# An instruction order put together stretch by stretch from twelve turns of a scheduler, in place of the best of eight turns

## The chip, the cores and the metric

The kernel runs on one core of a Trainium2 chip. The metric is the device time of one execution in microseconds (us). Three runs of the kernel before took 1519.48, 1521.61 and 1521.72 us; their median, 1521.61 us, is the time before.

## The reference

A two-layer encoder on 512 tokens of width 1024, all in float32. Each layer adds a normed token mixer and a normed SwiGLU to the stream:

```python
def reference(x, ...):
    for layer in range(DEPTH):                      # DEPTH = 2
        h = rms_norm(x, norm_mix_pre[layer])
        if layer % N_MIXERS == 0:
            h = neighbourhood_attention(h, ...)     # 8 x 64 token grid, window 8 x 16
        else:
            h = dilated_attention(h, ...)           # three (window, dilation) groups, merged
        x = x + rms_norm(h, norm_mix_post[layer])
        h = rms_norm(x, norm_ffn_pre[layer])
        x = x + rms_norm(swiglu(h, ...), norm_ffn_post[layer])
```

Layer 0 uses neighbourhood attention, layer 1 dilated attention; both have 16 heads of 64.

## The kernel before, in words

All large products are split into a high and a low part of float32r: `mm3` (L374 to L376) issues three matrix products for each wanted one. The projections of queries, keys, values and of the gate and up matrices go through a scheme with seven block products in place of eight (`Seven`, `Values`), whose sums are made by POOL and DVE and whose splits into high and low are made by ACT (L362) and DVE (L363).

The stages follow each other as: norm and transposes of the input; mixer 0 (eight pairs of heads; 0 to about 230 us); its output product `yo`; gate and up of layer 0 (`gu`, 22 units); the product down (`yd`); norm and transposes; the values of mixer 1 (`vd`), then eight pairs of heads of mixer 1 with three query/key units each (`pp_d`; about 730 to 1137 us); its output product; gate, up and down of layer 1.

Beside the float32r products, TensorE (PE) has 128x128 transposes (L748 to L755 in mixer 0, L1322 in mixer 1, L596 for operands) and a third kind: plain float32 products on half of the array. These are the products of probabilities and values (L766 in mixer 0; L1331 and L1337 in mixer 1) and the scores of two of the three dilated groups (L1264). Each of them shows in the profile as two records. An unbroken run of such half-array products on PE is called a **visit** below.

The order of the work is not the order of the Python code. After the whole program has been recorded, the class `Order` takes all instructions, gives each a cost in ns on its engine (`_cost`), links them by what they read and write and by the buffers they share (`link`), and computes an order for each of the five queues (PE, ACT, DVE, POOL, SP) by list scheduling (`run`). `run` knows three kinds of PE work and a cost `SWITCH` for a change of kind, and for 1000 ns of rank it stays with the kind it has (`stay`). `pin` makes a number of turns: a pass forward by rank gives start times, a pass backward from these gives new ranks, and so on. It keeps the order whose computed end is the earliest and pins it: each queue's instructions are chained one after the other (`add_manual_dep`). What runs on the chip is this fixed order on each queue. An engine whose next instruction is not ready waits, whatever else stands behind it.

SP issues the loads. In mixer 1 it also carries the merge weights of each pair of heads: a small array is written to `sw` in device memory (L1194) and read back into another layout by four small reads (L1196) each time. Between these stand the loads of later weights (L358), which wait until their buffer is free.

The lines that the steps below speak of, in short (L766 in `window_pv`, L1331 and L1337 in `values`, L1264 in `scores_b`, the others in `swapped` and in `Order.run`):

```python
pe.matmul(o[64 * hd:64 * hd + 64, q0:q0 + nq], v[:, kt, c:c + 64], pts[hd][:, p0:p0 + nq], ...)        # L766
rw = slice(64 * hd, 64 * hd + 64)
pe.matmul(ss[hd][:, f0:f0 + P], qf[rw, block(c)], kf[rw, block(c)], start=True, stop=True)             # L1264
pe.matmul(o[64 * hd:64 * hd + 64, q0:q0 + nq], vg[0][:, kt, c0:c0 + 64], pts[j, 0, hd][:, p0:p0 + nq], ...)  # L1331
nc.sync.dma_start(d[:, :4 * n], in_)                                                                   # L1194
for k in range(4):
    nc.sync.dma_start(out_[32 * k:32 * k + 32].rearrange(...), d[:, n * k:n * k + n].rearrange(...))   # L1196
...
heap = min((q for q in heaps[e] if q), key=lambda q: q[0])          # run: the lowest rank that is ready
for q in heaps[e][3:] if kind == 3 else heaps[e][kind:kind + 1]:
    if e == 0 and q and q[0][0] < heap[0][0] + self.stay:           # PE: the kind that it has, if near enough
        heap = q
```

Of the kernel before, what the change touches and what calls it, by code (L numbers as in the profile page):

```python
# [129 lines left out]
class Order:  # L130
# [145 lines left out]
                now = min(q[0] if q is wake else q[0][0] for q in (wake, pending) if q)  # L276
        return starts, order, max(s + max(c[1], c[4] and LANDING + c[4] / RATE) for s, c in zip(starts, self.costs))

    def pin(self, tc, times):
        rank, best = list(range(len(self.all))), None  # L280
        for _ in range(times):
            starts, order, end = self.run(rank, False)
            if best is None or end < best[0]:
                best = end, order
            starts, _, end = self.run([-s - c[1] for s, c in zip(starts, self.costs)], True)
            rank = [end - s - c[0] for s, c in zip(starts, self.costs)]
        for q in best[1]:
            for m, n in zip(q, q[1:]):
                tc.add_manual_dep(self.all[n], self.all[m].name,
                                  mybir.DependencyInfo(mybir.DependencyClass.NoSync, mybir.DependencyReason.DATA),  # L290
                                  reason="order")
        return best[0]


@with_exitstack
def encoder_kernel(ctx: ExitStack, tc: tile.TileContext, a: dict, out: bass.AP):
# [817 lines left out]
    for j in range(PAIRS):  # L1114
# [3 lines left out]
        q = next(q_).rearrange("p (h t) -> p h t", h=2)  # L1118
# [226 lines left out]
    order = [3 * j + g for j in range(PAIRS) for g in orders[j]]  # L1345
# [36 lines left out]
    for n, i in enumerate(order):  # L1382
# [7 lines left out]
        if g == 0:  # L1390
            q = q_.rearrange("p (h t) -> p h t", h=2)
# [34 lines left out]
              for n, lo, hi, o, c, side in arenas]  # L1426
    order = Order(tc.nc.cur_bb.bb.instructions)
    order.link(tags, places, extra)
    order.pin(tc, 8)


def _blocks(w, cols):
# [79 lines left out]
```

## Time and profile before

| | |
|---|---|
| median of three runs | 1521.61 us |
| profiled execution, its own time | 1517.54 us |
| span in that profile | 1515.8 us |
| PE busy | 1462.6 us, 96% of the span |
| DVE, ACT, POOL busy | 79%, 59%, 39% |
| share of the chain that ended last: PE, ACT, DVE, DMA | 70%, 4%, 4%, 2% |

The span is what the instructions cover; the execution's own time is 1.74 us more, and that execution was 4.07 us under the median of the runs. PE counts as busy while a matrix product is in its pipeline, so the busy share hides small losses between the starts of products; the timeline, which gives each start, shows them.

### The profile page before, as it was taken

What the parts mean: (1) busy time and instruction counts of PE and PEld (TensorE: products, weight loads), DVE (VectorE), ACT (ScalarE), POOL (GpSimd) and SP (SyncE); (2) the same over time, 40 slices, a digit from 0 to 9 for tenths busy, and PEclk for the clock granted to TensorE, in tenths of its full rate; (3) what the DMA queues carried; (4) which work ended last, traced back from release to release, by engine and by line L of the source; (5) the groups of instructions that cost most, each with busy time, mean ns of one, the idle gap of its engine ahead of it and who ended that gap; (6) DMA issues with size and microseconds to landing.
All of it is one profiled execution on the core that took longest, in us unless ns stands there. A gap on an engine that the chain in (4) does not pass through costs nothing.

```text
span 1515.8 us, 27980 instructions
## 1 busy us (share of the span) xinstructions
PE 1462.6 (96%) x10788; PEld 1355.0 (89%) x10788; DVE 1190.3 (79%) x1884; ACT 895.4 (59%) x1787; POOL 597.4 (39%) x484
## 2 busy tenths in 40 slices
PE   7999998999999999999999999999998999999997
PEld 7988876999999788999999988989986999999786
DVE  5389976898888789797578667877747988887876
ACT  4467764555555557544468667877764654555564
POOL 4356754543330001676464455454306433330001
PEclk9999999999999999999999999999998999999999
DMA  5356575756462774545334776672647232322762
GB/s 180 115 206 161 173 245 202 193 173 201 153 157 77 238 227 148 204 154 160 132 126 169 175 200 186 186 189 72 211 153 223 84 112 84 112 84 91 259 220 91
DMA packets 82118, 247.26 MB, mean 163 GB/s; under 512 B 18816, under 2 KB 29056, under 8 KB 79936
## 3 DMA queue, kind: packets, MB, share of 16 engines
q1 hardware_dynamic: 70064, 180.32, 35.7%
q0 software_dynamic: 11776, 64.88, 16.1%
q8 instruction: 85, 1.39, 0.4%
q14 instruction: 49, 0.40, 0.1%
q10 hardware_dynamic: 144, 0.26, 0.0%
HBM read 223.31 MB, written 68.26 MB: 192 GB/s over the span
## 4 chain that ended last, share of the span: by engine, by line
PE 70%; ACT 4%; DVE 4%; DMA 2%; issue 2%; POOL 1%; SPq 0%; POOLq 0%; DVEq 0%; ACTq 0%
PE gu L375 10%; PE gu L374 10%; PE gu L376 10%; PE pp_d L374 4%; PE pp_d L376 4%; PE pp_d L375 4%; PE yd_s L376 3%; PE yd_s L374 3%; PE yd_s L375 3%; PE yd_pp L375 2%; PE yd_pp L376 2%; PE yd_pp L374 2%; PE vd L374 2%; PE vd L376 2%; PE vd L375 2%
## 5 line engine op out<-in xcount | busy, mean ns | idle before, releaser
L375 PE MATMUL gu<-rxc,h_a 128*128 128x256 f32 x352 | 101.4, 288 | 2.9 <-DVE rxc L599 2.8
L376 PE MATMUL gu<-rxc,l_a 128*128 128x256 f32 x352 | 101.0, 287 | 0.2 <-DVE l_a L363 0.2
L374 PE MATMUL gu<-rxc,h_a 128*128 128x256 f32 x352 | 101.2, 290 | 0.0
L375 PE MATMUL gu<-rxa,h_b 128*128 128x256 f32 x352 | 99.8, 284 | 0.8 <-DVE rxa L599 0.8
L374 PE MATMUL gu<-rxa,h_c 128*128 128x256 f32 x352 | 100.3, 285 | 0.0
L374 PE MATMUL gu<-rxa,h_b 128*128 128x256 f32 x352 | 99.9, 284 | 0.0
L376 PE MATMUL gu<-rxa,l_b 128*128 128x256 f32 x352 | 99.7, 283 | 0.0
L375 PE MATMUL gu<-rxa,h_c 128*128 128x256 f32 x352 | 99.5, 283 | 0.0
L376 PE MATMUL gu<-rxa,l_c 128*128 128x256 f32 x352 | 99.4, 283 | 0.0
L442 POOL TENSOR_TENSOR fg<-fg 128x512 f32<-128x512 f32 x24 | 38.1, 1586 | 121.1 <-DVE l_a L363 105.6
L362 ACT ACTIVATE rxc<-hid 128x512 fp32r<-128x512 f32 (+1 forms) x84 | 49.3, 592 | 60.9 <-PE yd_pp L375 37.9
L442 POOL TENSOR_TENSOR r_gu<-r_gu 128x512 f32<-128x512 f32 x20 | 30.8, 1540 | 108.9 <-DVE l_a L363 94.4
L442 POOL TENSOR_TENSOR r_d<-r_d 128x512 f32<-128x512 f32 x24 | 36.8, 1533 | 92.3 <-DVE l_ad L363 38.6
L363 DVE TENSOR_TENSOR rxc<-hid,rxc 128x512 fp32r<-128x512 f32 (+1 forms) x84 | 53.7, 647 | 23.8 <-ACT rxc L362 22.0
L375 PEld LDWEIGHTS gu<-rxc,h_a 128*128 128x128 f32 x352 | 68.8, 196 | 3.5 <-DVE rxc L599 3.5
L1232 ACT ACTIVATE ap<-ap 128x256 f32<-128x256 f32 x128 | 63.8, 504 | 11.2 <-DVE ap L1231 11.0
L374 PEld LDWEIGHTS gu<-rxc,h_a 128*128 128x128 f32 x352 | 69.0, 197 | 0.5 <-ACT rxc L598 0.5
L376 PEld LDWEIGHTS gu<-rxc,l_a 128*128 128x128 f32 x352 | 68.8, 196 | 0.5 <-DVE l_a L363 0.5
L375 PEld LDWEIGHTS gu<-rxa,h_b 128*128 128x128 f32 x352 | 67.5, 192 | 1.0 <-DVE rxa L599 1.0
L572 POOL DMA_DIRECT2D hid<-g_ffn_post x2 | 1.2, 617 | 170.0 <-DVE rxc L363 170.0
L374 PEld LDWEIGHTS gu<-rxa,h_c 128*128 128x128 f32 x352 | 67.5, 192 | 0.8 <-DVE fg L838 0.4
L374 PEld LDWEIGHTS gu<-rxa,h_b 128*128 128x128 f32 x352 | 67.5, 192 | 0.2
(602 smaller groups left out, 6254.5 us busy)
## 6 DMA issues: line engine op xcount, KB each, us to landing
wsum<-wd POOLq DMA_DIRECT2D x24, 1408.0 KB, 11.5
r_d<-dil_qk SPq DMA_DIRECT2D x48, 512.0 KB, 4.5
fg<-wg SPq DMA_DIRECT2D x24, 512.0 KB, 3.8
fg<-wu SPq DMA_DIRECT2D x24, 512.0 KB, 5.1
wsum<-wsum POOLq DMA_DIRECT2D x8, 1408.0 KB, 7.7
raw<-wsum SPq DMA_DIRECT2D x22, 512.0 KB, 4.7
r_gu<-wg SPq DMA_DIRECT2D x20, 512.0 KB, 3.7
r_gu<-wu SPq DMA_DIRECT2D x20, 512.0 KB, 4.5
```

What stands on the lines that cost most here:

```text
L362: act.activation(h, src, AF.Copy)
L363: dve.tensor_sub(l, src, h.bitcast(F32))
L374: i = pe.matmul(o, s[0], m[0], start=start, stop=False, skip_group_check=True)
L375: pe.matmul(o, s[0], m[1], start=False, stop=False, skip_group_check=True)
L376: pe.matmul(o, s[1], m[0], start=False, stop=stop, skip_group_check=True)
L442: self.added = e[0].tensor_add(q[0], q[0], q[2])
L572: queue.dma_start(g, bass.AP(tensor=row.tensor, offset=row.offset, ap=[[0, P], [1, D]]))
L1232: act.activation(pr[:, f], pr[:, f], AF.Exp, bias=st[:, c:c + 1], scale=-1.0, accum_out=st[:, c + 2:c + 3])
```

## The change

`pin` makes twelve turns in place of eight and keeps, of each but the first, the computed end, the ranks, the start times and the order. It takes the turn with the earliest end as the base. Then it goes through the program in stretches of 50000 ns of the base's computed time. For each stretch and each other turn it replaces the ranks of the instructions that start in the stretch by that turn's ranks (moved by the median difference, so that they fit to the rest), runs the scheduler forward once more, and keeps the new order where its computed end is earlier. Instructions, tiles, costs and links stay as they are.

```diff
-    def pin(self, tc, times):
-        rank, best = list(range(len(self.all))), None
-        for _ in range(times):
+    def pin(self, tc, times, span):
+        rank, found = list(range(len(self.all))), []
+        for n in range(times):
             starts, order, end = self.run(rank, False)
-            if best is None or end < best[0]:
-                best = end, order
+            if n:
+                found.append((end, rank, starts, order))
             starts, _, end = self.run([-s - c[1] for s, c in zip(starts, self.costs)], True)
             rank = [end - s - c[0] for s, c in zip(starts, self.costs)]
-        for q in best[1]:
+        found.sort(key=lambda f: f[0])
+
+        best, rank, base, order = found[0]
+        for lo in np.arange(0.0, max(base), span):
+            part = [k for k, s in enumerate(base) if lo <= s < lo + span]
+            for _, other, _, _ in found[1:]:
+                mixed, shift = list(rank), float(np.median([rank[k] - other[k] for k in part]))
+                for k in part:
+                    mixed[k] = other[k] + shift
+                _, new, end = self.run(mixed, False)
+                if end < best:
+                    best, rank, order = end, mixed, new
+        for q in order:
...
-    order.pin(tc, 8)
+    order.pin(tc, 12, 5e4)
```

What it comes to: the order before is that of the eighth turn, and the base of the new one is the twelfth, with pieces of other turns in twelve of its thirty stretches. Of PE's 10388 products 8019 keep their place in the row, and no other moves by more than 100 places; of ACT's 1544 instructions 992 keep theirs, of DVE's 1676 it is 1112, of POOL's 480 it is 415, of SP's 467 it is 398. On PE the rows differ, with equal pieces between, at what was 76 to 220 us, 265 to 297, 604 to 626, 776 to 1138, 1176 to 1198 and 1327 to 1400 us of the profile; elsewhere they are the same. PE makes 82 visits in the order before (20 in mixer 0, 62 in mixer 1) and 67 in the new one (16 and 51). By the lines in a visit: L766 alone 20 and now 16, L1331 alone 13 and 9, L1337 alone 13 and 7, L1264 alone 23 and 21, mixed 13 and 14.

In the rows below, the line numbers of the changed kernel are greater by 12.

**PE, end of mixer 0.** `o_6` is the value product of the seventh pair, `ta`/`tb` are its neighbour's transposes, `s_15` the last head's scores. Before:

```order
L766 MATMUL o_6_2278<-ap_255,apv 64x192
L766 MATMUL o_6_2278<-ap_255,apv 64x256
L753 MATMUL tb_13_2267<-ident,ap_255 128x128
L754 MATMUL tb_13_2267<-ident,ap_255 128x128
L755 MATMUL tb_13_2267<-ident,ap_255 128x64
L766 MATMUL o_6_2278<-ap_255,apv 64x256 x2
L715 MATMUL s_15_1_2404<-rxc 128x256
L716 MATMUL s_15_1_2404<-rxc 128x256
L715 MATMUL s_15_1_2404<-rxc 128x256
L716 MATMUL s_15_1_2404<-rxc 128x256
L766 MATMUL o_6_2278<-ap_255,apv 64x256
L766 MATMUL o_6_2278<-ap_255,apv 64x192 x2
```

Now:

```order
L765 MATMUL tb_13_2267<-ident,ap_255 128x128
L766 MATMUL tb_13_2267<-ident,ap_255 128x128
L767 MATMUL tb_13_2267<-ident,ap_255 128x64
L727 MATMUL s_15_1_2404<-rxc 128x256
L728 MATMUL s_15_1_2404<-rxc 128x256
L727 MATMUL s_15_1_2404<-rxc 128x256
L728 MATMUL s_15_1_2404<-rxc 128x256
L778 MATMUL o_6_2278<-ap_255,apv 64x192 x2
L778 MATMUL o_6_2278<-ap_255,apv 64x256 x4
L778 MATMUL o_6_2278<-ap_255,apv 64x192 x2
```

The eight products of `o_6` stood in four visits (the first, of one product, is ten rows ahead of what is shown), and stand in one now, behind the scores.

**PE, mixer 1.** `pp_d` are the query/key products, `o_0` the values of the first pair, `sb` the scores of dilated groups. Before:

```order
L374 MATMUL pp_d_8940<-rxb_6344,h_bd_9073 128x256
L1337 MATMUL o_0_8478<-ap_6475 64x4x32
L1264 MATMUL sb_1_1_8832<-ap_6475 128x128
L1337 MATMUL o_0_8478<-ap_6475 64x4x32
L1264 MATMUL sb_0_0_9139<-ap_6475 128x128
L375 MATMUL pp_d_8940<-rxb_6344,h_bd_9073 128x256
```

Now, some 30 rows earlier:

```order
L388 MATMUL pp_d_8940<-rxa,l_ad_8955 128x256
L1276 MATMUL sb_0_1_8831<-ap_6475 128x128
L1276 MATMUL sb_1_1_8832<-ap_6475 128x128
L1349 MATMUL o_0_8478<-ap_6475 64x4x32 x8
L386 MATMUL pp_d_8781<-rxb_6344,h_bd_8901 128x256
```

Left-over products that stood by themselves have moved into the visit ahead.

**SP, mixer 1, fourth pair of heads.** `r_d` are weight buffers, `sw` the small array of the merge weights. Before:

```order
L358 DMA r_d_10213<-dil_qk 128x1024
L1194 DMA sw_6478<-ap_6475 128x16
L358 DMA r_d_10213<-dil_qk 128x1024
L1196 DMA ap_6475<-sw_6478 32x4x4 x4
L358 DMA r_d_10443<-dil_qk 128x1024 x2
L1194 DMA sw_6480<-ap_6475 128x8
```

Now:

```order
L370 DMA r_d_10213<-dil_qk 128x1024 x2
L1206 DMA sw_6478<-ap_6475 128x16
L370 DMA r_d_10443<-dil_qk 128x1024
L1208 DMA ap_6475<-sw_6478 32x4x4 x4
L370 DMA r_d_10443<-dil_qk 128x1024
L1206 DMA sw_6480<-ap_6475 128x8
```

One load of the next weights has moved from behind the group of four small reads to ahead of it. At six of the groups of mixer 1 at least one load has moved ahead in this way.

## Rows read from the trace of the kernel before

**Rows 1.** The page of the profile: the span, each engine's busy time, and the TensorE clock that was granted, in 40 slices (9 is 90% of full speed or more).
```profile
span 1515.8 us, 27980 instructions
PE 1462.6 (96%) x10788; PEld 1355.0 (89%) x10788; DVE 1190.3 (79%) x1884; ACT 895.4 (59%) x1787; POOL 597.4 (39%) x484
PEclk9999999999999999999999999999998999999999
```

**Rows 2.** Busy time of each engine in stretches of the span: the stretch, then us busy (and instructions) of PE, weight loads, DVE, ACT and POOL, the granted clock as a share of full speed, the share of the DMA engines, GB/s.
```profile
85.00:220.00 135.00, 131.14 (x950) 113.38 (x951) 122.72 (x298) 99.40 (x237) 90.77 (x108) 1.00 0.63 195
300.00:500.00 200.00, 199.85 (x1632) 198.07 (x1632) 175.51 (x226) 103.26 (x180) 61.49 (x41) 1.00 0.51 152
604.00:626.00 22.00, 21.35 (x180) 21.01 (x181) 19.03 (x24) 12.14 (x20) 15.16 (x11) 1.00 0.49 168
777.00:1000.00 223.00, 221.16 (x1834) 203.96 (x1834) 167.27 (x368) 156.12 (x400) 116.63 (x97) 1.00 0.65 183
1000.00:1137.00 137.00, 136.01 (x1071) 120.52 (x1069) 94.55 (x217) 103.18 (x263) 44.74 (x41) 1.00 0.52 157
1156.00:1172.40 16.40, 8.99 (x43) 7.89 (x42) 15.33 (x14) 6.80 (x12) 16.40 (x13) 0.69 0.59 225
1327.00:1400.00 73.00, 73.00 (x595) 72.11 (x594) 62.03 (x88) 38.91 (x67) 13.54 (x8) 1.00 0.26 85
```

**Rows 3.** What PE waited for: engine, tile and line that waited <- what it waited for: us in total, times, the longest.
```profile
PE tr_o L596 <- DVE rxc L599: 9.7, 2, 5.1
PE tr_a L596 <- DVE ea L589: 8.0, 1, 8.0
...
PE o L766 <- ACT ap L756: 0.8, 2, 0.4
...
PE t L1322 <- DVE ap L1323: 0.3, 1, 0.3
```

**Rows 4.** The timeline of PE around three visits of mixer 1: one product of L1331, two of L1337, twelve of L1337 (2, 4 and 24 records): start in us, us until the last end, what. The start-to-start times matter, since ends overlap.
```profile
828.76 0.28 PE L374 MATMUL pp_d<-rxa,h_cd 128*128 128x256 f32 x1
828.97 0.65 PE L1331 MATMUL o<-ap 128*64 128x256 f32 x2
...
829.77 0.28 PE L376 MATMUL pp_d<-rxa,l_cd 128*128 128x256 f32 x1
...
892.36 0.28 PE L376 MATMUL pp_d<-rxb,l_bd 128*128 128x256 f32 x1
892.48 0.28 PE L374 MATMUL pp_d<-rxb,h_bd 128*128 128x256 f32 x1
892.69 0.44 PE L1337 MATMUL o<-ap 128*64 128x128 f32 x4
...
893.28 0.28 PE L376 MATMUL pp_d<-rxb,l_bd 128*128 128x256 f32 x1
...
1033.97 0.28 PE L376 MATMUL pp_d<-rxa,l_cd 128*128 128x256 f32 x1
1034.18 1.53 PE L1337 MATMUL o<-ap 128*64 128x128 f32 x24
...
1035.86 0.28 PE L375 MATMUL pp_d<-rxa,h_cd 128*128 128x256 f32 x1
```

**Rows 5.** The same for two visits of mixer 0, one of seven products (14 records) and one of a single product (2 records).
```profile
201.15 0.39 PE L375 MATMUL yo<-l_wo,rxa 128*128 128x512 f32 x1
201.38 0.39 PE L376 MATMUL yo<-h_wo,rxa 128*128 128x512 f32 x1
201.70 1.73 PE L766 MATMUL o<-ap,apv 128*64 128x192 f32 x14
203.36 0.27 PE L748 MATMUL ta<-ident,ap 64*128 64x64 f32 x1
203.56 0.33 PE L749 MATMUL ta<-ident,ap 128*128 128x128 f32 x1
...
211.61 0.39 PE L376 MATMUL yo<-rxa 128*128 128x512 f32 x1
211.93 0.54 PE L766 MATMUL o<-ap,apv 128*64 128x192 f32 x2
212.40 0.27 PE L748 MATMUL ta<-ident,ap 64*128 64x64 f32 x1
212.60 0.33 PE L749 MATMUL ta<-ident,ap 128*128 128x128 f32 x1
```

**Rows 6.** The timeline of SP's queue in mixer 1: a load with a group of small reads issued right behind it, and the group of the fourth pair with the loads behind it.
```profile
835.57 0.33 SPq L358 DMA_DIRECT2D r_d<-dil_qk  x1
835.99 2.31 SPq L1196 DMA_DIRECT2D ap<-sw  x4
...
941.16 1.92 SPq L1196 DMA_DIRECT2D ap<-sw  x4
943.19 0.84 SPq L358 DMA_DIRECT2D r_d<-dil_qk  x2
```

**Rows 7.** DMA issues, KB each and median us from issue to landing: from the page, the loads of `r_d` over the whole span; from the stretch 805 to 840 us, the small reads that were issued at 835.99 us.
```profile
r_d<-dil_qk SPq DMA_DIRECT2D x48, 512.0 KB, 4.5
...
ap<-sw SPq DMA_DIRECT2D x4, 1.0 KB, 1.6
```

More of the change, by code (lines that the diff above doesn't have):

```diff
@@ L291, in pin @@
                                   reason="order")
-        return best[0]
+        return best
 @with_exitstack
```

## The prediction, as recorded before the changed kernel ran

> **What bounds the kernel now.** I read the page first. PE is busy for 1462.6 of 1515.8 us and the granted clock is near full in all slices [rows 1]; no other engine is above 79%. So the time is PE's row of products plus the places where PE waits. The stretches show where those places are: in gate and up (300 to 500 us, 1327 to 1400 us) PE idles for 0.15 us and not at all, while it idles for 3.86 us of 135 in mixer 0, 0.65 of 22 between the layers, 1.84 of 223 and 0.99 of 137 in mixer 1 [rows 2]. The largest single losses are transposes of operands that wait for DVE, 9.7 us in two waits and 8.0 us in one [rows 3]. The second of the two long ones lies in the stretch 1156 to 1172.4 us, where PE is busy for 8.99 of 16.4 us and the mean clock is 0.69, a mix of the two levels 2.4 and 1.2 GHz after PE had idled [rows 2]. The reader is to see that the new order leaves these transposes and the products around them in the same sequence, so that I count nothing there. What is left for a new order is small: 7.34 us of idle in the four stretches it changes (3.86 + 0.65 + 1.84 + 0.99), and what PE loses without showing idle, by changing its kind of work. For that I went to the timeline of PE and read start-to-start times.
>
> **The term that is certain: 15 visits fewer.** A product of 128x256 follows the one before it after 0.12 us (892.36 to 892.48) [rows 4]. Around a visit it is more. From the last full product ahead of a visit to the second one behind it I subtract the two full products themselves, 0.24 us.
> Two products of L1337: 892.48 to 893.28 is 0.80, less 0.24 is 0.56 us. Twelve of them: 1033.97 to 1035.86 is 1.89, less 0.24 is 1.65 us [rows 4]. The ten more cost 1.09, so 0.109 each, and 0.56 - 2 x 0.109 = 0.34 us belong to the visit and not to its products.
> In mixer 0, seven products of L766: 201.38 to 203.56 is 2.18 us; a single one: 211.61 to 212.60 is 0.99 us [rows 5]. The six more cost 0.198 each. The single one's 0.99 holds a `yo` product of 0.23 (as 201.15 to 201.38), a small transpose of 0.20 (212.40 to 212.60, as 203.36 to 203.56) and its own 0.198, which leaves 0.36 us for the visit.
> A single product of L1331: 828.76 to 829.77 is 1.01, less 0.24 is 0.77 us [rows 4]; it has 256 columns as most of L766's have, so by 0.198 for the product 0.57 us are the visit's.
> L1264 alone I did not price by a pair of its own; I take L1337's 0.34, the low end.
> By the lines of the visits that go: 4 x 0.36 (L766) + 4 x 0.57 (L1331) + 6 x 0.34 (L1337) + 2 x 0.34 (L1264), less 0.34 for the one mixed visit more, is 1.44 + 2.28 + 2.04 + 0.68 - 0.34 = **6.1 us**. The bounds are 15 x 0.34 = 5.1 and 15 x 0.57 = 8.6 us. The same products are still done; only the entering and leaving goes.
>
> **The term that is open: waits.** The new order does not make ACT, DVE or POOL faster, and their rows have moved too (552 of ACT's 1544 instructions, 564 of DVE's 1676). Where PE reaches a product sooner than its operand is there, the gain turns into a wait. In mixer 1 PE idles for 0.8% and 0.7% of the two stretches, and its transposes of probabilities waited for 0.3 us in all [rows 2, 3], so most of the gain there should stay. In mixer 0 PE idles for 2.9%, and a value product waited for ACT's copy [rows 2, 3]; this is the stretch in which DVE is busy for 122.72 of 135 us. There I take the gain of the four visits, 1.4 us, as given back. From both sides: if the idle of the four changed stretches went too, 7.3 us more would be gained; if each of the gains met a wait, all 6.1 would be lost.
>
> **Edits at nothing.** In 1327 to 1400 us only products of one kind change places and PE is busy for 73.00 of 73 us; the cover is that the operands lie ready, and if it goes the loss is a wait like those above. At 604 to 626 us some transposes change places with value products; PE idles there for 0.65 us, which bounds a gain, and a loss of that size is my bound on the other side. At 265 to 297 and 1176 to 1198 us transposes of the third and fourth token blocks move by a few products among `gu` products; by the same argument nothing.
> On SP, one load or more has moved ahead of the small reads of the merge weights at six places. Behind them wait DVE's weights and ACT's scaling, and behind these PE's transposes. The row shows that a group of small reads issued 0.42 us behind a 512 KB load had landed 1.6 us after its issue [rows 6, 7], so the load does not hold the reads back much once it is issued. What can hold them is the load's own wait for its buffer: at the fourth pair it was issued at 943.19, right behind reads issued at 941.16 [rows 6], so in the new row the reads could go out up to 2.0 us later. PE's wait of 0.3 us in all at these transposes [rows 3] is why I count nothing for it.
> The Trainium skill ("DMA: Bandwidth & Descriptors", "Queues, rings and completion order") says that on each DMA engine the descriptors of one queue are consumed in ring order, which speaks against this move: by it the reads would start behind the whole load. With the median of 4.5 us of such a load [rows 7] six places would be late by 27 us together before any cover; the 1.6 us above do not bear that out, and I go by the row.
>
> **The sum.** 6.1 - 1.4 = 4.7 us less. Against the profiled execution, 1517.54 us, that gives 1512.8. That execution lies 4.07 us under the median of the runs, and the forecast is for the median of runs: 1521.6 - 4.7 = **1516.9 us**.
>
> **Rivals.** A change of under 0.2%, 3.0 us, can hardly be told from none by measurements of this kernel.
> (a) *The gain turns into waits.* The twelve turns and their pieces are compared by computed costs, which may not be those of the chip; for it speaks that every third row of ACT and DVE has moved, against it that PE idles so little in mixer 1. If at least 1.7 us more of the 4.7 are given back, the result is within 0.2%; if all, 1521.6 us. Chance 0.28.
> (b) *The idle goes too.* In mixer 0 the order gathers the value products behind the scores, and a wait of 0.4 us for ACT ahead of a value product [rows 3] may go with it. Keeping all 6.1 and winning the larger part of 7.3 us, say 4, gives 1511.5 us. Chance 0.12.
> (c) *Merge weights late: slower.* At the six groups the reads go out 2.0 us later each [rows 6], 12 us in all, and PE's transposes of these pairs then wait for the scaled probabilities. With the 6.1 us won this is 5.9 us more, 1527.5 us. It decides from 9.1 us of such waits on (6.1 + 3.0). For it speaks that the load of the fourth pair went out right behind the reads [rows 6], which leaves open since when its buffer had been free; against it, the 0.3 us of waits before [rows 3]. Were the queue's ring order to hold the reads for the whole load, as the skill's page would have it, the loss would be larger still. Chance 0.12.
>
> **How the numbers follow.** My forecast, 1514 to 1518.6 us, has 0.48, (a) 0.28, (b) 0.12, (c) 0.12. The range runs from 1510 to 1524 us: it takes in (b) at 1511.5, the forecast with the visits at either bound (5.1 and 8.6), and (a) with a small loss; most of (c) stays out, which with the tails is no more than 2 in 10. Faster by over 0.2% are the forecast and (b): 0.60. Within 0.2% is (a): 0.28. Slower is (c): 0.12.
>
> **What would show it.** In the new profile, visits of one product should be rarer in the timeline between 85 and 1137 us, and the starts around a single one as far apart as before. PE's last product of the output of mixer 1 should start some 4 to 6 us earlier, with most of it won after 777 us; from there on both profiles should run alike, the waits for operands of 5 us and the low clock after them included. In the list of waits, `t` at L1322 should stay under 1 us; if it shows several us, with DVE's weights waiting longer for `sw`, (c) is at work. If visits have gone and PE's idle in the changed stretches has grown by as much, it is (a). If PE's stretch from 1198 us on starts later than before, the forecast is wrong.

## The result and the profile after

The changed kernel takes 1522.59 us (median of 20 runs; 1518.88 to 1525.75) against 1518.51 us for the kernel before on the same chip (20 runs; 1515.15 to 1521.76). The ratio is 1.0025 with a 95% interval of 1.0016 to 1.0035: about 4 us slower, where 4.7 us faster was forecast. The profiled execution of the changed kernel took 1523.31 us, its span is 1521.5 us. Line numbers of the changed kernel are 12 higher than those before, below `pin`.

The page of the changed kernel, span and PE's busy time [rows 1 before], with DVE, ACT and POOL:
```profile
span 1521.5 us, 27984 instructions
PE 1458.8 (96%) x10788; PEld 1353.5 (89%) x10788; DVE 1190.7 (78%) x1884; ACT 895.0 (59%) x1787; POOL 590.3 (39%) x484
```
With the same products PE is busy for 3.8 us less than before (1462.6), and the span is 5.7 us longer, so its waits have grown by more. Three of the stretches that [rows 2] showed, now:
```profile
85.00:220.00 135.00, 129.51 (x943) 112.31 (x944) 125.03 (x296) 96.29 (x227) 85.11 (x108) 1.00 0.63 187
...
777.00:1000.00 223.00, 215.28 (x1802) 200.80 (x1801) 166.52 (x354) 156.31 (x398) 114.04 (x95) 0.98 0.63 179
1000.00:1137.00 137.00, 135.10 (x1061) 121.58 (x1060) 94.50 (x229) 103.52 (x266) 46.82 (x44) 1.00 0.55 165
```
PE's idle has grown from 3.86 to 5.49 us in mixer 0, and from 1.84 to 7.72 us in 777 to 1000 us, where the mean clock has also fallen to 0.98. PE's waits (engine, tile and line, who ended it: total, times, longest) name what is new beside [rows 3]:
```profile
PE tr_o L608 <- DVE rxc L611: 9.4, 2, 5.2
PE tr_a L608 <- DVE ea L601: 8.2, 2, 7.9
...
PE pp_d L386 <- DVE pp_d L444: 2.7, 1, 2.7
PE yo L386 <- DMA rxa<-rvd: 2.4, 2, 1.5
```
The two long waits for transposes stand as they did. New are 2.7 us for a bank of `pp_d` that DVE had not released, and 2.4 us for operands of `yo` that came back late.

**Where the time went, stretch by stretch.** Both orders issue the same products, so one product's start can be subtracted between two profiles. I cut PE's row where both orders have issued the same set of products. The first columns give the stretch (its times in the kernel before) and the visits in it; the others how much longer than before the stretch took, in us. `e1`, `e5` and `e12` are experiments below.

| stretch | visits before, after | changed | e1 | e5 | e12 |
|---|---|---|---|---|---|
| 73 to 219 (mixer 0) | 19, 15 | +1.39 | +1.52 | +0.02 | +0.96 |
| 219 to 300 | 1, 1 | +0.43 | -0.24 | -0.11 | +0.61 |
| 300 to 602 (gate, up, down) | 0, 0 | +0.61 | -1.01 | -1.59 | -1.04 |
| 602 to 776 | 0, 0 | -0.06 | -0.45 | +0.02 | -0.12 |
| 776 to 821 (mixer 1) | 4, 4 | +1.05 | +1.07 | +0.03 | +1.07 |
| 821 to 905 | 15, 10 | -3.26 | -3.71 | -2.16 | -3.30 |
| 905 to 925 | 4, 4 | +0.35 | +0.34 | +0.33 | +1.83 |
| **925 to 967** | 8, 6 | **+6.03** | -0.69 | -0.70 | -0.91 |
| 967 to 1012 | 9, 7 | -1.04 | -1.51 | -1.58 | -1.53 |
| 1012 to 1110 | 20, 18 | -1.47 | -1.40 | -1.54 | -1.42 |
| 1110 to 1121 (output) | 0, 0 | +1.84 | +1.65 | +0.03 | +0.03 |
| 1121 to 1203 | 2, 2 | +0.35 | +0.68 | +0.55 | +0.90 |
| 1203 to 1327 | 0, 0 | -0.01 | -0.01 | +0.01 | 0.00 |
| 1327 to 1418 | 0, 0 | -0.35 | -0.34 | -0.35 | -0.33 |

In mixer 1 the stretches with fewer visits are shorter, apart from the one at the fourth pair, which loses 6 us. Mixer 0 is longer although four visits have gone; it, the start of mixer 1 and the output product lose 1 to 2 us each.

**The stretch 925 to 967 us, read backward from PE.** PE's row (start, length, and in brackets the idle time with its releaser):
```profile
952.27 1.49 PE L1276 MATMUL sb<-ap 64*128 64x128 f32 x16
956.46 0.39 PE L386 MATMUL pp_d<-rxb,h_bd 128*128 128x256 f32 x1 [2.70 <-DVE pp_d L444]
...
959.04 0.58 PE L386 MATMUL pp_d<-rxb,h_cd 128*128 128x256 f32 x1 [0.88 <-DVE ap L692]
959.41 0.42 PE L387 MATMUL pp_d<-rxb,h_cd 128*128 128x256 f32 x1
959.63 0.42 PE L388 MATMUL pp_d<-rxb,l_cd 128*128 128x256 f32 x1
```
PE waits for DVE's clearing of a `pp_d` bank (L444). DVE's row:
```profile
944.38 0.67 DVE L375 TENSOR_TENSOR rxc<-r_d,rxc 128x512 fp32r<-128x512 f32 x1
955.31 0.17 DVE L1224 TENSOR_TENSOR ap<-ap 128x8 f32<-128x8 f32 x1 [10.27 <-DMA ap<-sw]
...
955.59 0.41 DVE L687 SCALAR_TENSOR_TENSOR ap<-pp_d,ap 128x256 f32<-128x256 f32 x1
...
956.13 0.27 DVE L444 MEMSET pp_d<- 128x256 f32 x1
```
DVE stands for 10.27 us at the first operation of the fourth pair's weights, which waits for the last of four small reads of `sw`, and the evacuation (L687) and clearing (L444) of PE's bank are queued behind it. SP's row there [rows 6 before]:
```profile
943.18 0.33 SPq L370 DMA_DIRECT2D r_d<-dil_qk  x1
943.63 1.96 SPq L1208 DMA_DIRECT2D ap<-sw  x4
945.65 0.43 SPq L370 DMA_DIRECT2D r_d<-dil_qk  x1
```
And when they landed. These are issues of 943.1 to 945.6 us, KB each and us from issue to landing: the load and POOL's transfer to `wsum` that was issued at 944.24 us, then of the four reads the first, the second and the last by themselves.
```profile
wsum<-wd POOLq DMA_DIRECT2D x1, 1408.0 KB, 13.4
r_d<-dil_qk SPq DMA_DIRECT2D x1, 512.0 KB, 4.0
...
ap<-sw SPq DMA_DIRECT2D x1, 2.0 KB, 3.9
...
ap<-sw SPq DMA_DIRECT2D x1, 2.0 KB, 9.8
```
In the kernel before the four landed 1.7 us after their issue (median):
```profile
ap<-sw SPq DMA_DIRECT2D x4, 2.0 KB, 1.7
```
The reads went out 2.5 us later than before (943.63 against 941.16), behind the load that now stands ahead of them and that had itself waited 5.8 us for its buffer. The first two landed right behind the load (947.54 and 947.98 us; the load 947.17), the last one at 955.12 us. And the clock (stretch, PE busy, then the other engines; the last three columns are granted clock, DMA share and GB/s):
```profile
952.00:956.00 4.00, 1.76 (x24) 1.40 (x18) 0.66 (x4) 0.00 (x0) 0.00 (x0) 1.00 0.92 236
956.00:959.00 3.00, 1.62 (x5) 1.03 (x5) 2.95 (x8) 1.65 (x3) 0.00 (x0) 0.62 0.08 23
959.00:963.00 4.00, 3.96 (x18) 3.96 (x19) 3.22 (x9) 1.71 (x5) 1.73 (x2) 0.50 0.16 59
963.00:970.00 7.00, 7.00 (x59) 6.83 (x58) 5.71 (x11) 5.25 (x15) 4.22 (x5) 0.96 0.86 290
```
Behind the wait PE works at 0.50, the lower of its two levels, until about 963.5 us. At that level a full product follows another after 0.22 us (959.41 to 959.63) instead of the 0.12 of [rows 4]. Against the same stretch without this wait (-0.69 us, e1) 6.7 us were lost: 3.6 us to PE's two waits, and most of the remaining 3 us to the clock.

### The profile page after: what moved, and what is told of

Same layout as the page of the kernel before. It is cut to its first block, busy times and chain, and to the rows that moved or that the text cites. A ratio compares the mean times of both kernels' runs of the same rounds, so it can differ in the third digit from the quotient of the medians.

```text
span 1521.5 us, 27984 instructions
## 1 busy us (share of the span) xinstructions
PE 1458.8 (96%) x10788; PEld 1353.5 (89%) x10788; DVE 1190.7 (78%) x1884; ACT 895.0 (59%) x1787; POOL 590.3 (39%) x484
## 3 DMA queue, kind: packets, MB, share of 16 engines
q8 instruction: 85, 1.39, 0.4%
## 4 chain that ended last, share of the span: by engine, by line
PE 70%; DVE 5%; DMA 3%; ACT 2%; issue 2%; POOL 1%; SPq 0%; POOLq 0%; DVEq 0%; ACTq 0%
PE gu L387 9%; PE gu L386 9%; PE gu L388 9%; PE pp_d L386 5%; PE pp_d L388 4%; PE pp_d L387 4%; PE yd_s L388 3%; PE yd_s L387 3%; PE yd_s L386 3%; PE yd_pp L387 2%; PE yd_pp L388 2%; PE yd_pp L386 2%; PE vd L386 2%; PE vd L388 2%; PE vd L387 2%; PE t L1334 2%
## 5 line engine op out<-in xcount | busy, mean ns | idle before, releaser
L388 PEld LDWEIGHTS gu<-rxa,l_b 128*128 128x128 f32 x352 | 67.5, 192 | 0.1
```

The costliest lines, as they stand in the source:

```text
L388: pe.matmul(o, s[1], m[0], start=False, stop=stop, skip_group_check=True)
```

## The experiments

Each kernel pins the five rows from tables: `OLD` are the rows of the kernel before, `NEW` those of the changed kernel, as numbers of instructions; `move` takes some out of a row and puts them back ahead of or behind another. The diffs show the edit of these rows. Times are medians beside runs of the kernel before on the same chip (1518.05 to 1518.31 us in the four sets); ratios are to that kernel, with the 95% interval.

### The load back behind the reads (e1)

```diff
 q = [list(x) for x in NEW]
+q[SP] = move(q[SP], [9422], after=9053)    # load of r_d17's first half, behind the four reads
```


> The changed order with one row moved: SP's load of r_d17's first half, 512 KB, goes back behind the four small reads of the fourth pair. Theory A (the load ahead of the reads is the loss: reads late, DVE stands in the weights, PE's bank pp_d16 is released late): the reads land within 4 us of their issue instead of 3.9 to 9.8 us, DVE's 10.3 us of waiting there falls under 4 us, PE's 2.7 us wait for pp_d goes with the low clock behind it, and the time falls by 5 to 6 us, to 1516.5 to 1518 us. Theory B (PE has run ahead of ACT and DVE and would stand about here whatever the reads do): the reads land early, PE waits for something else for about as long, and the time stays within 1 us of 1522.6 us. Theory C (POOL's transfer to wsum of 1408 KB, issued 1.3 us earlier than before, holds the reads): the reads still land 6 us or more after their issue, and the time stays within 1.5 us of 1522.6 us.

Measured: 1517.59 us, 0.9995 (0.9984 to 1.0007). One row of SP's 467 moves, and 5.0 us come back by the medians (4.6 by the two ratios, 1.0025 and 0.9995). The fourth pair's reads, and PE's stretch behind them:
```profile
ap<-sw SPq DMA_DIRECT2D x4, 2.0 KB, 1.8
```
```profile
952.00:956.00 4.00, 4.00 (x36) 4.00 (x35) 3.33 (x7) 3.09 (x8) 3.60 (x4) 1.00 0.64 160
```
The reads land 1.8 us after issue, PE does not idle in 952 to 956 us, and the stretch 925 to 967 us is 0.69 us shorter than before instead of 6.03 longer. Theory A holds and B falls: PE's lead met no other wait here. C is not yet separated, since POOL's transfer now starts behind the reads.

### The load ahead in the old order (e2)

```diff
 q = [list(x) for x in OLD]
+q[SP] = move(q[SP], [9422], before=9050)
```


> The order of the kernel before with the same one row moved the other way: the load of r_d17's first half ahead of the four reads of the fourth pair. Theory A: the reads are issued about 2.4 us later (943.6 us) and land 4 to 10 us after their issue instead of 1.7 us, DVE stands several us at the weights, and the time is 2 to 6 us over the kernel before. Theory B: the old order has no lead of PE to lose, and the time stays within 1 us of the kernel before. Theory C: the wsum transfer stays behind the reads on the clock, so the reads land within 3 us of their issue, and the time rises by 1 us or less.

Measured: 1519.39 us, 1.0012 (0.9998 to 1.0026): the interval holds no change. In the profile the stretch 925 to 967 us is 1.69 us longer. The fourth pair's reads, and then DVE's wait for them and PE's wait behind it:
```profile
ap<-sw SPq DMA_DIRECT2D x4, 2.0 KB, 3.8
```
```profile
DVE ap L1212 <- DMA ap<-sw: 4.6, 1, 4.6
...
PE pp_d L374 <- DVE ap L680: 1.1, 1, 1.1
```
The load alone makes reads of 1.7 us into reads of 3.8 us, and costs a quarter of what it costs in the new order. Here `wsum` was issued at 943.70 us, behind the last read. So A names a part of the loss, and something of the new order makes up the rest.

### POOL's transfer later (e3)

```diff
 q = [list(x) for x in NEW]
+q[POOL] = move(q[POOL], [9563], after=9514)    # wsum, behind the two additions for r_d16
```


> The changed order with one row moved on POOL: the transfer to wsum of 1408 KB (issued at 944.24 us) goes behind the two additions for r_d16 that followed it, to about 948 us; SP's load stays ahead of the reads. Theory A: the reads still lie behind the load; the last lands 4 to 7 us after its issue rather than 9.8, and 1 to 4 us of the 6.4 us lost between 952 and 957 us come back (1518.5 to 1521.5 us). Theory B: no change within 1 us. Theory C: the reads land within 2.5 us of their issue, and the time falls by 5 to 6 us, to 1516.5 to 1518 us.

Measured: 1516.94 us, 1.0001 (0.9989 to 1.0013). The load stays ahead of the reads, `wsum` goes out at 947.66 us:
```profile
r_d<-dil_qk SPq DMA_DIRECT2D x2, 512.0 KB, 4.0
ap<-sw SPq DMA_DIRECT2D x4, 2.0 KB, 3.6
```
The reads still lie 3.6 us, as behind the load in e2, and not under the 2.5 us of C. But none lies 7 to 10 us any more, DVE waits for 3.6 us instead of 10.3, and PE's stretch is as short as in e1 (-0.91). So neither A nor C alone is right: the load ahead makes 2 us of late issue and 2 us of late landing, which DVE's row can bear in the new order; the transfer between the reads makes 6 us more of the last one, which it cannot. Taking away either is enough.

### DVE's release ahead of the weights (e4)

```diff
 q = [list(x) for x in NEW]
+q[DVE] = move(q[DVE], [9359, 9360, 9383, 9447], before=9097)    # d16's evacuation, clearing, two splits
```


> The changed order with four rows moved on DVE: the evacuation and clearing of pp_d16 and the two splits behind them (L444 and the three before and after it in DVE's row) go ahead of the first operation of the fourth pair's weights; SP and POOL as in the changed kernel. Theory A: the reads land as late as in the changed kernel (the last 8 us or more after its issue), but PE's wait of 2.7 us for pp_d at 953.7 us goes, and 3 to 6 us come back (1516.5 to 1519.5 us), less if PE then waits for the probabilities that need the weights. Theory B: the time stays within 1 us of 1522.6 us. Theory C does not differ from A here.

Measured: 1520.51 us, 1.0017 (1.0005 to 1.0029); the stretch 925 to 967 us is 2.13 us longer than before instead of 6.03. The last read still took 10.3 us, PE's wait for the clearing is gone, and a wait for the next operations of DVE's row takes its place:
```profile
PE pp_d L374 <- DVE ap L680: 2.0, 1, 2.0
```
It confirms the way from the reads to PE, through DVE's row. In the stretch 3.9 us came back, as expected; the median fell by 2 us only. The rest isn't explained by a run: in this profile three stretches with spells of low clock are 1.3 to 1.8 us longer than before (905 to 925, 1121 to 1203, 1327 to 1418 us), against 0.35, 0.35 and -0.35 us in that of the changed kernel.

### The new order where it gained (e5, e6)

```diff
+CUT = ((5718, 7792, 8500), (742, 1190, 1300), (861, 1245, 1400), (295, 402, 440), (231, 339, 380))
+take = (OLD, NEW, OLD, NEW)    # to 822 us, to 1112 us, to 1250 us, to the end
+q = [sum((t[e][a:b] for t, a, b in zip(take, (0,) + CUT[e], CUT[e] + (None,))), []) for e in range(5)]
+q[SP] = move(q[SP], [9422], after=9053)
```


> The new order only between 822 and 1112 us (17 of PE's visits fewer and 6 more there, 11 net) and behind 1250 us, with the load of r_d17's first half behind the reads as in the run before; the old order in mixer 0, in 776 to 822 us, and from 1112 to 1250 us, POOL's rows from 1077 us on among it. Theory D (the effect of the new order is a sum of pieces, each read from PE's starts in the changed kernel and in the run with the load put back): 822 to 905 us -3.5, 905 to 925 +0.35, 925 to 967 -0.8, 967 to 984 +0.5, 984 to 1012 -2.05, 1012 to 1110 -1.45, behind 1327 -0.35, together -7.3 us against the kernel before, so 1510.5 to 1511 us if the wait of 1.4 us for rxa behind 1110 us goes with POOL's old rows, 1512.5 us if PE meets it because it comes early. Theory E (the lead of PE is given back further on, since ACT, DVE and the transfers are not faster): within 2 us of the kernel before.

Measured: 1512.29 us, 0.9957 (0.9940 to 0.9973), 6.0 us under the kernel before: the fastest of all. The pieces of 822 to 1112 us come to -5.7 us and that behind 1327 us to -0.35 (table, e5), against the 7.3 expected; 821 to 905 us gave 2.16 and not 3.5: in the whole new order part of that stretch's gain only makes good the 1.05 us lost just ahead of it (776 to 905 us together are -2.21 there and -2.13 here). The wait behind 1110 us is gone. Theory E falls: the lead is not given back.

e6 differs by POOL's rows from 1077 to 1117 us (413 in place of 402 in `CUT`).


> As the run at 822 to 1112 us, but POOL's rows from 1077 to 1117 us in the new order: the write of rvd ahead of a scaling, the reads of rxa in another sequence. If POOL's rows make PE's wait for rxa behind 1110 us, this run shows 1.4 to 1.8 us of it and is that much longer than the one with POOL's old rows; if PE's early arrival makes it, both show it, and they agree within 0.5 us in the starts of PE at 1121 us.

Measured: 1513.88 us, 0.9964 (0.9952 to 0.9977). The stretch 1110 to 1121 us is +0.03 us as in e5, so neither POOL's rows nor PE's early arrival make that wait; what both have in common is the old rows of PE, ACT, DVE and SP behind 1112 us. e12 tests 18 products of PE's row alone.

### Mixer 0 in the old order (e7), in halves (e10, e11)

```diff
+CUT = ((2500,), (400,), (500,), (200,), (150,))
+take = (OLD, NEW)    # to 400 us, to the end; and the load of r_d17 behind the reads as in e1
```


> The changed order with the load put back behind the reads and mixer 0 (to 300 us) in the old order. By PE's starts in the changed kernel the new mixer 0 costs 1.3 to 1.9 us although it has four visits fewer, so theory D expects PE at 300 us 1.3 to 1.9 us earlier than in the run with the load alone put back, and the time at 1516 us, 2 us under the kernel before. If the four visits were worth the 1.4 us of my prediction and the rest was chance, PE would be 1.4 us later at 300 us.

Measured: 1517.18 us, 0.9989 (0.9977 to 1.0001), which can't be told from e1. By PE's starts 73 to 219 us take 0.29 us more than before instead of 1.52, so 1.2 us of mixer 0's loss are gone there, and 0.65 us of it by 300 us, where theory D expected 1.3 to 1.9; further on 776 to 821 us took 2.45 us more in this execution where e1 had 1.07, and the low clock came three times.

e10 takes PE's row of mixer 0 alone from the new order, e11 the other four rows alone:

```diff
 q = [list(x) for x in OLD]
+q[PE] = NEW[PE][:2500] + OLD[PE][2500:]                                                # e10
+q = [NEW[e][:c] + OLD[e][c:] for e, c in enumerate((0, 400, 500, 200, 150))]    # e11
```


> The kernel before with PE's row of mixer 0 alone in the new order (four visits fewer), the rows of ACT, DVE, POOL and SP as before. In the changed kernel 73 to 146 us cost 0.85 us more and 146 to 219 us 0.6 us more. If PE's own sequence makes the loss (it comes to products sooner than ACT and DVE have their operands), both stretches are at least that much longer here too, 1.4 us or more together. If the moved rows of the other engines make it, PE keeps the gain of its visits here: 1.4 to 2.6 us less by 219 us.

> The counterpart: the kernel before with the rows of ACT, DVE, POOL and SP of mixer 0 in the new order, PE's row as before. If the moved rows of the others make the loss, 73 to 219 us are 1 to 3 us longer here; if PE's sequence makes it, they stay within 0.3 us.

Measured: e10 1520.30 us, 1.0018 (1.0008 to 1.0029), 73 to 219 us +1.29; e11 1521.50 us, 1.0016 (1.0004 to 1.0029), +1.84. Each half alone costs as much as both together (+1.39). Rows that were computed together do not fit when one is exchanged, so this pair can't say which half makes the loss. That stays open. What is shown is the place: in 85 to 220 us PE of the changed kernel waits 1.2 us for ACT ahead of a small transpose, 1.1 us at a `pp_n` product for ACT and 0.8 us at `yo` for a transfer of `rxa`, none of which the kernel before has.

### SP's whole row as before (e8)

```diff
+return NEW[:SP] + [OLD[SP]]
```


> The changed order with SP's whole row as before, so the loads behind the reads at all six places, not at the fourth pair alone. Theory A, in which only the fourth pair's reads hold PE: PE's starts as in the run with that load alone put back, within 0.5 us in each stretch, and the time within 1 us of its 1517.6 us. If the other five places cost too (reads that landed 4 to 7 us after their issue at 964.7, 1088.8 and 1119.6 us), 1 to 4 us less, most of it behind 984 us.

Measured: 1529.13 us, 1.0068 (1.0051 to 1.0086). Neither theory: 11 us slower than e1. Behind 984 us each stretch is within 1 us of e1, so the loads at the other places cost nothing there. But the old row of SP fits the new rows of the other engines badly at two places that the edit was not aimed at. In mixer 0 PE waits 3.3 us (a load of `r_n` is late). And at the third pair SP's old row has a load ahead of the reads, with `wsum` issued at 902.17 us between the second and the third; the first and the third read by themselves, then the waits of DVE and PE from 900 to 920 us, and the stretch behind them (granted clock 0.56):
```profile
ap<-sw SPq DMA_DIRECT2D x1, 2.0 KB, 3.6
...
ap<-sw SPq DMA_DIRECT2D x1, 2.0 KB, 8.5
```
```profile
DVE ap L1212 <- DMA ap<-sw: 7.9, 1, 7.9
...
PE pp_d L374 <- DVE ap L683: 4.5, 1, 4.5
```
```profile
909.00:916.00 7.00, 4.25 (x20) 3.47 (x20) 2.65 (x9) 4.08 (x8) 0.00 (x0) 0.56 0.18 60
```
The same chain as at the fourth pair, at a second place, with the low clock behind it: reads behind a load, a POOL transfer between them, DVE standing, PE's bank late.

### The price of a visit by itself (e9)

```diff
 q = [list(x) for x in OLD]
+for inside, full in SPLIT:                     # ten visits of mixer 1
+    q[PE] = move(q[PE], [full], before=inside)    # the full product behind a visit into its middle
```


> The kernel before with ten visits of mixer 1 cut in two: the full product that follows a visit is put into its middle (at 831, 837, 840, 891, 896, 938, 1021, 1026, 1034 and 1052 us; three of L1264, one of L1264 with L1337, four of L1337, three of L1331 lines), so ten visits more and nothing else moved. It measures the price of a visit by itself. By the predictions's 0.34 to 0.57 us a visit, 3.4 to 5.7 us more; by the run of the new order in 822 to 1112 us, where 11 visits fewer went with 7 us less, 0.65 us a visit, 6.5 us more, 1524.5 us. If the gain there came from something else (fewer waits, other rows), less than 2 us more, with PE's starts apart by nothing around a cut visit.

Measured: 1521.34 us, 1.0018 (1.0008 to 1.0027), 3.1 us more. Around the ten places PE's starts are further apart by 0.35 us six times, and by 0.39, 0.50, 0.52 and 0.55 us at the other four: 4.05 us together, 0.41 us a visit. By kind (there are two L1264 visits among the ten, at 831 and 1052 us, not three): 0.35 at each of the three L1331 visits, 0.50 and 0.39 at L1264, 0.35 three times and 0.52 at L1337, 0.55 at the mixed one. The twelve products of L1337 of [rows 4], now in two visits of six:
```profile
1035.67 0.28 PE L376 MATMUL pp_d<-rxa,l_cd 128*128 128x256 f32 x1
1035.88 0.88 PE L1337 MATMUL o<-ap 128*64 128x128 f32 x12
1036.69 0.38 PE L374 MATMUL pp_d<-rxa,h_cd 128*128 128x256 f32 x1
1037.00 0.88 PE L1337 MATMUL o<-ap 128*64 128x128 f32 x12
1037.81 0.39 PE L375 MATMUL pp_d<-rxa,h_cd 128*128 128x256 f32 x1
1038.03 0.28 PE L376 MATMUL pp_d<-rxa,l_cd 128*128 128x256 f32 x1
```
From 1035.67 to 1038.03 us is 2.36 us. Before it was 1.89 from the product ahead to the second one behind, and here one full product more lies between (0.12): 2.36 - 0.12 - 1.89 = 0.35 us for one visit more.

### The products of `yo` in their old sequence (e12)

```diff
 q = [list(x) for x in NEW]
 q[SP] = move(q[SP], [9422], after=9053)
+q[PE][7820:7838] = OLD[PE][7820:7838]    # 18 products of yo
```


> The changed order with the load put back behind the fourth pair's reads, and 18 products of yo on PE (1117 to 1121 us in the profile before) in their old sequence: those of the operand in rxa that comes back last are the sixteenth and later again, not the first. In the changed kernel and in the run with the load alone put back, PE stood 1.4 to 1.5 us there for the transfer rxa from rvd, and the stretch of 10.4 us was 1.65 to 1.84 us longer. If PE's sequence makes that wait, the stretch is back within 0.3 us of 10.43 and the time 1.7 us under the run with the load alone put back, 1515.9 us. If the transfer is late for any sequence, since PE arrives 6 us earlier, 1 us or more of it stays.

Measured: 1515.62 us, 0.9981 (0.9971 to 0.9991). The stretch 1110 to 1121 us is +0.03 us instead of +1.65, and PE waits for nothing in it. In the changed kernel the new sequence puts the product that needs the last part of `rxa` ahead of eleven that need nothing more, and PE stands:
```profile
1120.44 0.39 PE L386 MATMUL yo<-h_wo,rxa 128*128 128x512 f32 x1
1122.36 0.47 PE L386 MATMUL yo<-rxb,rxa 128*128 128x512 f32 x1 [1.53 <-DMA rxa<-rvd]
```

## Why the prediction was wrong, point by point

**What bounds the kernel: right.** PE's row is the time. Every difference found is a visit less, a wait of PE more, or PE at the lower clock behind a wait.

**The visits, 6.1 us: the price was right, the place only in part.** Ten visits by themselves cost 0.41 us each (e9), inside the 0.34 to 0.57 us taken from [rows 4, 5]; 15 times that is 6.1 us. That the sum agrees so well is partly luck: L1331, taken at 0.57, came out at 0.35, and L1264, taken at 0.34 without a row of its own, at 0.39 and 0.50. The 0.36 of mixer 0 has no run of its own. In mixer 1, with 11 visits fewer, 822 to 1112 us came out 5.7 us shorter (e5), 0.51 a visit. That is about 1 us more than the price of e9 gives (4.5 us), and no run shows where it comes from.

**Mixer 0's gain given back, 1.4 us: mis-sized.** Not only was the gain of four visits lost there, the stretch came out 1.4 us longer. Between the same two products (73 to 219 us) PE idles for 6.9 us where it idled for 5.0: the three new waits make 3.1 us, and some old ones are gone. That is 1.9 us of idle and 1.4 us of time, so only 0.5 of the 1.44 us from the visits shows; why not more stays open (e10, e11). By the same kind of wait 1.05 us went at 776 to 821 us (PE for DVE at a `pp_d` bank, 1.1 us) and 1.84 us behind 1110 us (`yo`), neither of which the sum had. That is rival (a), in three places, for 4.3 us together. Of the three, `yo` is settled by an experiment of its own (e12); at 776 to 821 us the loss is gone where that part of the order is the old one (e5), but which row makes it was not tested.

**"Edits at nothing", SP's loads moved ahead of the small reads: this is the step that failed.** I said that the load does not hold the reads back much once issued, from a read time of 1.6 us. That row did not belong to the reads I named. The reads of [rows 7] with 1.0 KB were issued at 816.55 us, with no load right ahead of them. Those issued at 835.99 us, 0.42 us behind a 512 KB load [rows 6], are the ones of 2.0 KB, so [rows 7] is headed wrongly. This is POOL's transfer just ahead of them, and then their row in the kernel before (issues of 835 to 838 us):
```profile
834.37 1.22 POOL L870 DMA_DIRECT2D wsum<-wd  x1
```
```profile
wsum<-wd POOLq DMA_DIRECT2D x1, 1408.0 KB, 11.8
r_d<-dil_qk SPq DMA_DIRECT2D x1, 512.0 KB, 9.9
ap<-sw SPq DMA_DIRECT2D x4, 2.0 KB, 9.6
```
The right row said 9.6 us, with the same three things together as at the fourth pair: a load, the reads, and a transfer to `wsum`. Here the transfer was issued first, and the load took 9.9 us with the reads, so this row could not have told the load's part from the transfer's. Neither DVE nor PE waited for it. So the trace had the price of the three together, and I weighed the Trainium skill's rule of ring order ("DMA: Bandwidth & Descriptors", "Queues, rings and completion order") against the wrong number and set it aside. The runs agree with the rule: in e2 and e3 the reads land 3.6 to 3.8 us after issue (medians), as the load ahead of them, and 1.8 us with the load behind in e1; the first read landed 0.2 to 0.6 us behind the load in e2, in e3 and in the changed kernel. The same section says that a DMA engine takes turns between the queues that have work, a packet at a time; that fits the last read, which goes from 3.1 us in e3 to 9.8 us where POOL's transfer starts between the reads, but no run shows that turn-taking is the reason. The other half of that paragraph of mine held: the load waited for its buffer until 943.18 us, and with it the reads, 2.0 us longer than their data in `sw` needed (941.58 us).

**The way to PE: also wrong.** I looked for PE's transposes `t` (L1322) as those who wait, and priced them by their 0.3 us [rows 3]. The late reads reach PE another way: behind the waiting weights in DVE's row lies the release of a `pp_d` bank, which has nothing to do with the weights. e4 shows it by moving that release ahead: PE's wait for the clearing goes, and 3.9 of the 6.0 us with it.

**Rival (c) had the late reads right, and their way to PE, their size and their count wrong:** one place of six, not six of 2.0 us each, and 6.7 us there (6.03 against -0.69 in e1), half of it waits and the other half mostly the clock behind them. The gain of mixer 1's visits came, and with it the pieces add up to the 4.1 us measured: -5.7 in 822 to 1112 us, -0.35 behind 1327 us, +6.7 at the fourth pair, +1.4 in mixer 0, +1.8 at `yo` come to 3.9 us (the 1.05 us ahead of 821 us come back in the next stretch). I gave (c) a chance of 0.12.

**Single profiles and medians.** e1's profiled execution is 4.3 us shorter than that of the kernel before (1513.23 against 1517.54), its median only 0.5 (interval -2.4 to +1.1): 1.0 us of the 4.3 is in 300 to 602 us, where the kernel before had a spell of low clock and e1 had none (last section). The spread of single executions is wide enough for the rest (1513.23 to 1521.93 us in e1). The stretches that repeat over four and more profiles carry the argument, not the ends. The same holds for my base: the median of three runs was 1521.61 us, that of twenty beside the changed kernel 1518.51. So 1522.59 us lies inside the range I gave, 1510 to 1524, by luck: moved down by these 3.1 us the range ends at 1520.9, below the measured time, and the change was slower where I forecast faster.

## What to carry to other kernels

Price a moved transfer by what is queued behind its first waiter, on that engine's row, and not by the one who needs the data: ten microseconds of DVE standing at an 8-column operation held back a clearing that PE needed. In this kernel a small read that shares a queue with 512 KB loads and the DMA engines with another queue's 1408 KB transfer took 1.7 or 9.8 us for the same 2 KB; which of the two depends on what was issued in the 2 us around it, so look up each issue by its own time before citing its row. An order made of pieces can be taken apart again at the points where both orders have done the same work, and the good pieces kept: the new order between 822 and 1112 us and behind 1250 us alone, with one load put back, ran 6 us faster than the kernel before.

## What the runs showed of the hardware that was not expected

The same short wait of PE is followed by low clock in one execution and not in another. In e3 and in e1 PE waits 1.4 us for DVE ahead of a score product and is busy for 4.6 of the 6 us from 914 to 920 us. Behind it, e3 and e1 (granted clock is the third number from the end):
```profile
914.00:920.00 6.00, 4.63 (x36) 4.05 (x34) 5.88 (x11) 3.49 (x11) 4.82 (x5) 1.00 1.01 343
920.00:923.60 3.60, 3.60 (x17) 3.34 (x17) 3.46 (x12) 3.55 (x8) 1.64 (x2) 0.53 0.57 235
```
```profile
914.00:920.00 6.00, 4.62 (x33) 3.89 (x33) 5.87 (x17) 3.99 (x9) 3.52 (x4) 1.00 1.01 343
920.00:923.60 3.60, 3.60 (x32) 3.59 (x31) 3.48 (x8) 3.60 (x10) 1.83 (x1) 1.00 0.19 78
```
It is worth 1.5 us: 905 to 925 us took 1.84 us more than before in e3 and 0.34 in e1. Three places behind such waits showed it, near 508, 921 and 1412 us, in some executions and not in others; near 508 us the kernel before and the changed one have it, e1, e5 and e12 have not, and in 300 to 602 us they are 1 to 1.6 us shorter than the kernel before. It is likely part of why runs of one kernel spread: e1's two fastest executions (1513.23 and 1513.51 us) have a mean granted clock of 0.993, its two slowest (1521.93 and 1521.44 us) 0.989.
